# The first two down-projection tiles moved into the pools of the stage before, and four input differences moved behind the third tile's weights

## The chip, the cores and the metric

The kernel runs on one NeuronCore of a Trainium2 chip. It uses five engines that run side by side and meet only at semaphores: TensorE (PE) multiplies matrices into PSUM, ScalarE (ACT) and VectorE (DVE) work on elements, GpSimd (POOL) and SyncE (SP) here mostly issue DMAs. The metric is the device time of one execution in microseconds, the median of several runs.

## The reference

One decoder layer on 512 prompt tokens and 32 sample tokens (544 columns in all), width 1024. What matters here is its last part, the MLP with 4096 hidden units; the two mixers before it (a state-space branch and a gated recurrence) are not touched.

```python
x = x + rms_norm(merged @ w_out, norm_mix_post)
h2 = rms_norm(x, norm_mlp_pre)
m = jnp.square(jax.nn.relu(h2 @ w_up)) @ w_down
x = x + rms_norm(m, norm_mlp_post)
```

All of it is float32.

## The kernel before, in words

**A product in three passes.** Activations and weights are held transposed, 128 features per partition. Each fp32 operand is cut into a high part (ScalarE casts it to the matmul's format) and a low part (VectorE subtracts the high part from the original). A product is then high times high, high times low and low times high, added up in PSUM. So each weight tile of 128x1024 needs three steps before TensorE can use it: a DMA of 512 KB (`wt`), a cast on ScalarE (`wh`) and a subtraction on VectorE (`wl`). A full output tile has 8 operand chunks, 3 passes and 2 halves of 272 columns: 48 matmuls, in 24 pairs.

**The MLP in chunks.** The hidden units come in four chunks of 1024. The first is made in the plain way: up projections u0 to u7 of `h2x`, each followed by relu and square, cut into `a0h` and `a0l` (eight operands, 0 to 7). Then come the eight down tiles d0_0 to d0_7 of this chunk, whose results are copied from PSUM into `ov`. The chunks after it are made with a Strassen-like scheme: sums and differences of weight quarters (names A, S12, S34, B) times sums and differences of input quarters. The input's part of that are four differences of quarters of `ov`, which holds the normalized `h2` until the copies of the down tiles overwrite it. Each difference has 128x1088 elements and is cut into high and low parts: `tb[1]` (t1h, t1l), `tb[2]` (t2h, t2l), `tb[3]` (in the place of bh and bl of the second half) and `tb[4]` (t).

**Pools.** The stage up to u7 takes its weights from pool `wts` (three load buffers `wt`, two each of `wh` and `wl`) and pool `res`. When these end, pool `up` takes their memory: six load buffers, four `wh` and four `wl`. A tile of `up` that lies over a tile of an older pool waits until that one is no longer used. PSUM has two tiles for full outputs, taken in turn, so a tile's first matmul waits until the result two tiles before has been copied out.

**Order.** Up to u7 a scheduler orders each engine's work by data and priorities (`tc.high_priority`). From the differences on, the order of all five queues is that of the code (`tc.manual_schedule`). In the code before, d0_0 and d0_1 are loaded and cut from pool `up` ahead of that block (L1401 to L1406), the four differences follow, and two of them are written in place into `ov`. The splits of tb[3] and tb[4] come before d0_1's matmuls, those of tb[1] and tb[2] after.

Of the kernel before, what the change touches and what calls it, by code (L numbers as in the profile page):

```python
# [9 lines left out]
F32 = mybir.dt.float32  # L10
F32R = mybir.dt.float32r
# [34 lines left out]
def layer(ctx, tc, a, o):  # L46
# [113 lines left out]
    def views(t):  # L160
        return [(halves(hi), halves(lo)) for hi, lo in t]
# [977 lines left out]
    with tc.tile_pool(name="res", bufs=5, reuse_waits="tile") as rp:  # L1139
# [92 lines left out]
        for k in (6, 7):  # L1232
# [4 lines left out]
            with tc.high_priority(offset=EAHEAD):  # L1237
                act_full(ps, k, f"u{k}")
        nc.gpsimd.dma_start(out=x1_d, in_=x1)
    wts.close()  # L1240
    ax = views(ah_)

# [2 lines left out]


    with tc.tile_pool(name="up", bufs=1, reuse_waits="tile") as up:
        tb = {n: tuple(up.tile([P, 4, HT], F32R, tag=f"t{n}{p}", name=f"t{n}{p}") for p in "hl") for n in (1, 2)}  # L1250
        tb[3] = hb[1, 0]
        t4 = big.tile([P, 2, 4, HT], F32R, tag="yhg", name="t4")
        tb[4] = (t4[:, 0], t4[:, 1])
        flat = lambda z: z.rearrange("p a b -> p (a b)")

        def raw(src, name):
            t = up.tile([P, 1024], F32, tag="wt", name=f"wt_{name}", bufs=6)
            if src is not None:
                nc.sync.dma_start(out=t, in_=src)
            return t  # L1260

# [111 lines left out]
        def d_load(c, m):  # L1373
            src = flat(a["w_down"][c, m]) if c < 3 else a["w_down2"][0, m].rearrange("p a b c -> p (a b c)")
            D[c, m] = raw(src, f"d{c}_{m}")

        def d_cut(c, m):
            D[c, m] = cut(D[c, m], f"d{c}_{m}")
# [19 lines left out]
            else:  # L1398
                tt(mv, ps[:, :, 0:HT], mv, ADD)

        with tc.high_priority(offset=WAHEAD):  # L1401
            for m in range(2):
                d_load(0, m)
                d_cut(0, m)
                d_rest(0, m)
            d_load(0, 2)  # L1406
        with tc.manual_schedule(engines={ET.PE, ET.Activation, ET.DVE, ET.SP, ET.Pool}):

            f11, f21, f12, f22 = (ov[:, 4 * kh:4 * kh + 4, HF[hf]] for hf in range(2) for kh in range(2))
            tt_ = [up.tile([P, 4, HT], F32, tag="t", name=f"tt{i}", bufs=2) for i in range(2)]  # L1410
            tt(tt_[0], f11, f12, SUB)
            stt(tt_[1], tt_[0], -1.0, f22, MUL, SUB)
            tt(f12, f22, f12, SUB)
            stt(f21, tt_[1], -1.0, f21, MUL, SUB)
            d_part(0, 0, *range(8))
            split(*tb[3], f12)
            split(*tb[4], f21)
            d_part(0, 1, *range(8))
            d_load(0, 3)
            d_cut(0, 2)  # L1420
            d_rest(0, 2)
            split(*tb[1], tt_[0])
            d_out(0, 0)
            split(*tb[2], tt_[1])
            d_out(0, 1)
            for c in range(3):

                ms = range(2 if c == 0 else 0, 8)
                q = 4 * c + 4
                nxt = {3: [lambda: load_a(q), lambda: load_s12(q), lambda: load_s34(q), lambda: load_b(q)],  # L1430
                       5: [lambda: add_s(q), lambda: hi("A", q), lambda: lo("A", q), lambda: load_a(q + 1)],
                       6: [lambda: hi("S12", q), lambda: lo("S12", q), lambda: load_s12(q + 1)],
                       7: [lambda: hi("B", q), lambda: lo("B", q), lambda: load_s34(q + 1), lambda: load_b(q + 1)]}
                for m in ms:
                    if m + 2 < 8 and not (c == 0 and m + 2 < 4):
                        d_load(c, m + 2)
                    if m + 1 < 8:
                        if m and not (c == 0 and m + 1 < 3):
                            d_cut(c, m + 1)
                            d_rest(c, m + 1)  # L1440
                    if c == 0 or m > 1:
                        d_part(c, m, *range(8))
                    elif m == 0:
                        d_part(c, 1, *range(6))
                        d_part(c, 0, 6, 7)
                    else:
                        d_part(c, 1, 6, 7)
                    for f in nxt.get(m, ()):
                        f()
                    d_out(c, m)  # L1450

                P1(q)
                keep("c1", q)
                P2(q)
                res(q)
                hi("S34", q)
                lo("S34", q)
                hi("A", q + 1)
                c11(q)
                lo("A", q + 1)  # L1460
                P5(q)
                load_a(q + 2)
                for p in range(q, q + 4):
                    n, nn, e = p + 1 < q + 4, p + 2 < q + 4, p == q + 3
                    P6(p)
                    if p > q:
                        hi("B", p)
                        act_hi(p - 1, 0)
                        lo("S34", p)
                    keep("u2", p)  # L1470
                    if p > q:
                        lo("B", p)
                        act_lo(p - 1, 0)
                    if nn:
                        load_s12(p + 2)
                    if n:
                        P1(p + 1)
                        keep("c1", p + 1)
                        add_s(p + 1)
                    if nn:  # L1480
                        load_s34(p + 2)
                        load_b(p + 2)
                    if not n:
                        d_part(c + 1, 0, 0, 1)
                    P7(p)
                    keep("u3", p)
                    c22(p)
                    if n:
                        hi("S12", p + 1)
                        P2(p + 1)  # L1490
                        res(p + 1)
                        c11(p + 1)
                        lo("S12", p + 1)
                    else:
                        d_part(c + 1, 0, 2, 3)
                    row1_a(p)
                    if nn:
                        hi("A", p + 2)
                    if not n:
                        d_cut(c + 1, 1)  # L1500
                        d_rest(c + 1, 1)
                    P4(p)
                    row1_b(p)
                    if nn:
                        lo("A", p + 2)
                    P3(p)
                    act_hi(p, 1)
                    c12(p)
                    row0(p)
                    if p + 3 < q + 4:  # L1510
                        load_a(p + 3)
                    if n:
                        hi("S34", p + 1)
                        P5(p + 1)
                    act_lo(p, 1)
                    if p == q + 1:
                        d_load(c + 1, 0)
                    if p == q + 2:
                        d_load(c + 1, 1)
                        d_cut(c + 1, 0)  # L1520
                        d_rest(c + 1, 0)
                act_hi(q + 3, 0)
                act_lo(q + 3, 0)
                if c < 2:
                    d_part(c + 1, 0, 4, 5)

            wd = []
            xr = {}
            w47 = big.tile([P, 4, 2, 512], F32R, tag="yhg", name="wd47")
            for m in range(8):  # L1530
                t = mp.tile([P, 2, 512], F32R, tag=f"bl{m // 2}{m % 2}", name=f"wd{m}") if m < 4 else w47[:, m - 4]
                wd.append((t[:, 0], t[:, 1]))
            wt = {}
            for m in range(8):
                j = m // 2
                if m % 2 == 0:
                    if j < 2:
                        d_load(3, j + 2)
                    if 0 < j < 3:
                        d_cut(3, j + 1)  # L1540
                        d_rest(3, j + 1)
                    wt[j] = raw(a["w_down2"][1, j].rearrange("p a b c -> p (a b c)"), f"e{j}")
                if m:
                    d_part(3, m, *range(4))
                if m % 2:
                    for i in range(2):
                        split(*wd[m - 1 + i], wt[j][:, 512 * i:512 * i + 512])
                d_out(3, m)
                if m > 3:
                    hf, kh = divmod(m - 4, 2)  # L1550
                    xr[hf, kh] = mp.tile([P, 4, HT], F32, tag=f"bh{hf}{kh}", name=f"xr{hf}{kh}")
                    nc.sync.dma_start(out=xr[hf, kh], in_=x1_d[:, 4 * kh:4 * kh + 4, HF[hf]])
# [152 lines left out]
```

## Time and profile before

| | |
|---|---|
| median of three runs | 980.4 us (980.24 to 983.28) |
| profiled execution, its own time | 980.57 us |
| its span, first to last instruction | 978.5 us |
| TensorE busy | 950.3 us, 97% of the span |
| VectorE busy | 621.5 us, 64% |
| ScalarE busy | 446.1 us, 46% |
| GpSimd busy | 62.5 us, 6% |
| mean granted TensorE clock | 0.991 of full speed |
| moved by DMA | 121.26 MB, 124 GB/s on average |

Of the profiled execution's time 2.1 us lie outside the span. Busy shares are averages over the whole program; what a stage waits for is read from that stage. In timelines, a bracket at a row's end gives the idle time of the engine just before it and what ended it. Matmul ends are modelled, so the step from one pair of matmuls to the next is read from their starts.

### The profile page before, as it was taken

How to read it: one execution, taken by the hardware profiler on the slowest of the kernel's cores; microseconds unless marked ns; L12 is line 12 of the kernel's file. 1: busy time of each engine (PE TensorE's matmuls, PEld its weight loads, DVE VectorE, ACT ScalarE, POOL GpSimd, SP SyncE). 2: the span in 40 equal slices, each digit the busy share in tenths (PEclk: the TensorE clock that was granted, in tenths of full speed). 3: DMA queues.
4: the chain of work that ended last, by engine and by line, in shares of the span. 5: the costliest groups of instructions: out<-in, count | busy, mean ns of one | idle time of the engine just before them, and what ended most of it. 6: DMA issues, size and time to landing. Idle time of an engine off the chain costs nothing.

```text
span 978.5 us, 21347 instructions
## 1 busy us (share of the span) xinstructions
PE 950.3 (97%) x9120; PEld 927.0 (95%) x9120; DVE 621.5 (64%) x1158; ACT 446.1 (46%) x834; POOL 62.5 (6%) x104
## 2 busy tenths in 40 slices
PE   8999999999999999999999999889999999999995
PEld 5999999989999999999999999889999999999994
DVE  6877669496684867657458567443564476347747
ACT  6744363544536323563334566333463165216623
POOL 2100000000000000612100000000100110010000
PEclk9999999999999999999999999989999999999998
DMA  7342242141423437565422512334453454346502
GB/s 257 97 134 68 65 149 76 65 137 59 143 67 103 135 131 262 189 211 181 137 88 87 191 28 111 130 98 113 111 176 98 119 144 132 103 119 166 184 2 91
DMA packets 45406, 121.26 MB, mean 124 GB/s; under 512 B 9120, under 2 KB 12576, under 8 KB 44672
## 3 DMA queue, kind: packets, MB, share of 16 engines
q1 hardware_dynamic: 37664, 97.20, 30.4%
q0 software_dynamic: 7360, 22.15, 8.8%
q8 instruction: 71, 1.16, 0.5%
q10 hardware_dynamic: 288, 0.56, 0.2%
q14 instruction: 23, 0.19, 0.1%
HBM read 101.66 MB, written 17.06 MB: 121 GB/s over the span
## 4 chain that ended last, share of the span: by engine, by line
PE 91%; DVE 4%; ACT 2%; issue 1%; DMA 1%; SPq 0%; DVEq 0%; ACTq 0%
PE ps_in L116 27%; PE ps_d L116 17%; PE ps_u L1311 7%; PE ps_u L126 7%; PE ps_bh L116 5%; PE ps_uy L1311 4%; PE ps_o L116 2%; PE ps_e L126 2%; PE ps_o L126 2%; PE ps_bs L116 2%; PE psL L643 2%; PE ps_uz L1311 2%; PE ps_u L116 1%; PE psO L709 1%; PE psK L693 1%
## 5 line engine op out<-in xcount | busy, mean ns | idle before, releaser
L116 PE MATMUL ps_in<-hh,wh_in 128*128 128x272 f32 x736 | 159.2, 297 | 0.0
L116 PE MATMUL ps_in<-hl,wh_in 128*128 128x272 f32 x736 | 153.0, 289 | 0.0
L116 PE MATMUL ps_in<-hh,wl_in 128*128 128x272 f32 x736 | 152.3, 288 | 0.0
L116 PEld LDWEIGHTS ps_in<-hh,wh_in 128*128 128x128 f32 x736 | 115.4, 189 | 2.9 <-issue 1.6
L116 PEld LDWEIGHTS ps_in<-hl,wh_in 128*128 128x128 f32 x736 | 115.7, 189 | 0.0
L116 PEld LDWEIGHTS ps_in<-hh,wl_in 128*128 128x128 f32 x736 | 115.6, 188 | 0.0
L71 DVE TENSOR_TENSOR wl_in<-wt_in,wh_in 128x1024 fp32r<-128x1024 f32 (+1 forms) x54 | 61.6, 1143 | 60.5 <-ACT wh_in L99 58.0
L116 PE MATMUL ps_d<-a0h,wl_d 128*128 128x272 f32 x448 | 94.5, 293 | 4.8 <-DVE wl_d L71 4.8
L116 PE MATMUL ps_d<-a0h,wh_d 128*128 128x272 f32 x448 | 94.0, 291 | 3.6 <-ACT wh_d L1264 3.2
L116 PE MATMUL ps_d<-a0l,wh_d 128*128 128x272 f32 x448 | 94.5, 293 | 0.0
L99 ACT CAST wh_in<-wt_in 128x1024 fp32r<-128x1024 f32 x46 | 48.3, 1052 | 98.0 <-PE ps_in L116 93.5
L116 PEld LDWEIGHTS ps_d<-a0h,wl_d 128*128 128x128 f32 x448 | 71.3, 190 | 6.0 <-DVE wl_d L71 5.7
L116 PEld LDWEIGHTS ps_d<-a0h,wh_d 128*128 128x128 f32 x448 | 71.4, 191 | 4.0 <-ACT wh_d L1264 3.4
L116 PEld LDWEIGHTS ps_d<-a0l,wh_d 128*128 128x128 f32 x448 | 71.5, 192 | 0.0
L71 DVE TENSOR_TENSOR ov<-ps_d,ov 128x544 f32<-128x544 f32 x24 | 17.4, 724 | 61.7 <-PE ps_d L116 61.7
L71 DVE TENSOR_TENSOR wl_d<-wt_d,wh_d 128x1024 fp32r<-128x1024 f32 x28 | 34.1, 1219 | 27.0 <-ACT wh_d L1264 27.0
L1264 ACT CAST wh_d<-wt_d 128x1024 fp32r<-128x1024 f32 x28 | 29.1, 1046 | 29.6 <-PE ps_d L116 23.6
L71 DVE TENSOR_TENSOR wl_S<-wt_S,wh_S 128x1024 fp32r<-128x1024 f32 x24 | 29.3, 1219 | 11.4 <-ACT wh_S L1264 11.4
L1264 ACT CAST wh_S<-wt_S 128x1024 fp32r<-128x1024 f32 x24 | 25.2, 1050 | 10.1 <-PE ps_d L116 10.1
L676 DVE COPY_PREDICATED scT<-masks,psL 32x128 f32<-32x128 uint8 x80 | 28.3, 354 | 2.3 <-PE psS L646 0.2
L116 PE MATMUL ps_bh<-yl,wh_bh 128*128 128x272 f32 x128 | 26.8, 291 | 1.4 <-DVE yl L71 1.4
L116 PE MATMUL ps_bh<-yh,wh_bh 128*128 128x272 f32 x128 | 27.1, 293 | 0.0
(546 smaller groups left out, 2324.9 us busy)
## 6 DMA issues: line engine op xcount, KB each, us to landing
wt_in<-in_w_in SPq DMA_DIRECT2D x52, 512.0 KB, 3.6
wt_d<-in_w_down SPq DMA_DIRECT2D x28, 512.0 KB, 3.9
wt_A<-in_w_up SPq DMA_DIRECT2D x12, 512.0 KB, 4.0
wt_S<-in_w_up SPq DMA_DIRECT2D x24, 256.0 KB, 2.7
wt_S<-in_w_up POOLq DMA_DIRECT2D x24, 256.0 KB, 4.4
s<-in_hg_s SPq DMA_DIRECT2D x8, 512.0 KB, 4.3
out_hg_s<-s SPq DMA_DIRECT2D x8, 512.0 KB, 3.7
wt_bh<-in_w_br_hg SPq DMA_DIRECT2D x8, 512.0 KB, 3.5
```

Source lines behind the costliest of these rows:

```text
L71: (e or V).tensor_tensor(out=out, in0=x, in1=y, op=op)
L99: S.copy(wh, wt)
L116: mm(ps[:, i, 0:int(np.prod(x[i].shape[1:]))], lhsT=w[:, c], rhs=x[i], start=st, stop=sp)
L126: mm(ps[:, i, 0:HT], lhsT=ws[i][j][:, c], rhs=x[hf], start=st, stop=sp)
L643: mm(pq[sq * y:sq * y + m, 4 * i + w], lhsT=k[:, i, c:c + m], rhs=up(c, c + sq, i), start=True, stop=True)
L676: V.copy_predicated(blocks(sc[r], h)[:, :, y, :, 1], masks[r, L].rearrange("p x (n h) -> p x n h", h=h), pq[r].rearrange("p x (n h) -> p x ...
L693: mm(pk[:, w], lhsT=kt2[:, i, w], rhs=vt[:, i, w], start=True, stop=True)
L709: mm(po[:, w], lhsT=sc[:, i, c], rhs=vt[:, i, w], start=True, stop=(w == 0))
L1264: S.copy(h, t)
L1311: mm(ps, lhsT=w[:, c], rhs=x_[:, k], start=(first and k == 0 and j == 0), stop=(k == 3 and j == 2), skip_group_check=True)
```

## The change

The first two down tiles, d0_0 and d0_1, are loaded, cut and multiplied in the stage of the older pools, with the helper `weights` that serves u6 and u7, right behind u7. Their matmuls keep their place. In the manual block their PSUM tiles are only taken over; the third tile's cut is written first, then the four differences. None of these is written in place any more: the first two keep their buffers (tag `t`), the third and fourth take two of the six load buffers of `up`, which grow from 1024 to 1088 columns. The copy of d0_0 comes before the split of tb[3], that of d0_1 before the split of tb[4], and the splits of tb[1] and tb[2] come in the rounds of the third and fourth tile.

```diff
+        ax = views(ah_)
+        first_d = []
+        for m in range(2):
+            wh, wl = weights(a["w_down"][0, m], f"d0_{m}")
+            first_d.append(dense_tile(f"ps_d0_{m}"))
+            dense(first_d[m], wh, wl, ax)
     wts.close()
-    ax = views(ah_)
...
         def raw(src, name):
-            t = up.tile([P, 1024], F32, tag="wt", name=f"wt_{name}", bufs=6)
-            if src is not None:
+            t = up.tile([P, 1088], F32, tag="wt", name=f"wt_{name}", bufs=6)
+            if src is not False:
+                t = t[:, 0:1024]
+            if src is not None and src is not False:
...
-        with tc.high_priority(offset=WAHEAD):
+        tb = {3: hb[1, 0]}
+        with tc.manual_schedule(engines={ET.PE, ET.Activation, ET.DVE, ET.SP, ET.Pool}):
             for m in range(2):
-                d_load(0, m)
-                d_cut(0, m)
-                d_rest(0, m)
-            d_load(0, 2)
-        with tc.manual_schedule(engines={ET.PE, ET.Activation, ET.DVE, ET.SP, ET.Pool}):
-
-            f11, f21, f12, f22 = (ov[:, 4 * kh:4 * kh + 4, HF[hf]] for hf in range(2) for kh in range(2))
-            tt_ = [up.tile([P, 4, HT], F32, tag="t", name=f"tt{i}", bufs=2) for i in range(2)]
-            tt(tt_[0], f11, f12, SUB)
-            stt(tt_[1], tt_[0], -1.0, f22, MUL, SUB)
-            tt(f12, f22, f12, SUB)
-            stt(f21, tt_[1], -1.0, f21, MUL, SUB)
-            d_part(0, 0, *range(8))
-            split(*tb[3], f12)
-            split(*tb[4], f21)
-            d_part(0, 1, *range(8))
-            d_load(0, 3)
+                PD[0, m] = first_d[m]
+                d_load(0, m + 2)
             d_cut(0, 2)
             d_rest(0, 2)
-            split(*tb[1], tt_[0])
+
+            f11, f21, f12, f22 = (ov[:, 4 * kh:4 * kh + 4, HF[hf]] for hf in range(2) for kh in range(2))
+            tf = {n: up.tile([P, 4, HT], F32, tag="t", name=f"tf{n}", bufs=2) for n in (1, 2)}
+            for n in (3, 4):
+                tf[n] = raw(False, f"tf{n}").rearrange("p (a b) -> p a b", a=4)
+            tt(tf[1], f11, f12, SUB)
+            stt(tf[2], tf[1], -1.0, f22, MUL, SUB)
+            tt(tf[3], f22, f12, SUB)
+            stt(tf[4], tf[2], -1.0, f21, MUL, SUB)
             d_out(0, 0)
-            split(*tb[2], tt_[1])
+            split(*tb[3], tf[3])
...
             d_out(0, 1)
+            split(*tb[4], tf[4])
...
+                    if c == 0 and m < 4:
+                        split(*tb[m - 1], tf[m - 1])
                     d_out(c, m)
```

How this moves the instructions is seen on three queues. ScalarE first, from the end of u6 on, before the change: `t_u` is the relu of an up tile (first u6's, then u7's), `a0h` its cast, `wh_d` the casts of the down tiles' weights, `bh`, `t` and `t1h` the high parts of the differences.

```order
L1205 ACTIVATE t_u_7975<-ps_u_7926 128x544
L1219 ACTIVATE e_7250<-psv_7992,eps_v 128x272
L132 CAST a0h_7263<-t_u_7975 128x544
L1205 ACTIVATE t_u_8050<-ps_u_8001 128x544
L132 CAST a0h_7265<-t_u_8050 128x544
L1264 CAST wh_d_0_8068<-wt_d_0_8066 128x1024
L132 CAST bh_6965<-ov 128x1088
L1264 CAST wh_d_1_8074<-wt_d_1_8072 128x1024
L132 CAST t_8065<-ov 128x1088
L1264 CAST wh_d_2_8192<-wt_d_2_8078 128x1024
L132 CAST t1h<-tt_8082 128x1088
L1397 COPY ov<-ps_d_0_8088 128x544
```

And ScalarE from the same place after the change:

```order
L99 CAST wh_d_0_8058<-wt_d_0_8056 128x1024
L1205 ACTIVATE t_u_7975<-ps_u_7926 128x544
L1219 ACTIVATE e_7250<-psv_7992,eps_v 128x272
L132 CAST a0h_7263<-t_u_7975 128x544
L99 CAST wh_d_1_8113<-wt_d_1_8111 128x1024
L1205 ACTIVATE t_u_8050<-ps_u_8001 128x544
L132 CAST a0h_7265<-t_u_8050 128x544
L1267 CAST wh_d_2_8177<-wt_d_2_8173 128x1024
L1400 COPY ov<-ps_d_0_8062 128x544
L132 CAST bh_6965<-wt_tf_8183 128x1088
L1400 COPY ov<-ps_d_1_8117 128x544
L132 CAST t_8192<-wt_tf_8184 128x1088
```

The casts of d0_0 and d0_1 moved ahead of the relus of u6 and u7, the third tile's cast follows a0h of u7 directly, and the two copies out of PSUM now stand ahead of the splits of the third and fourth difference.

VectorE from the last square of the up stage on, before the change: `t_u` is the square of u7, `a0l` its low part, `tt` and `ov` the four differences, `wl_d` the low parts of the down tiles' weights.

```order
L71 TENSOR_TENSOR t_u_8050<-t_u_8050 128x544
L71 TENSOR_TENSOR a0l_7266<-t_u_8050,a0h_7265 128x544
L71 TENSOR_TENSOR tt_8082<-ov 128x1088
L74 SCALAR_TENSOR_TENSOR tt_8083<-tt_8082,ov 128x1088
L71 TENSOR_TENSOR ov<-ov 128x4x272
L74 SCALAR_TENSOR_TENSOR ov<-tt_8083,ov 128x4x272
L71 TENSOR_TENSOR wl_d_0_8070<-wt_d_0_8066,wh_d_0_8068 128x1024
L71 TENSOR_TENSOR bl_6966<-ov,bh_6965 128x1088
L71 TENSOR_TENSOR wl_d_1_8076<-wt_d_1_8072,wh_d_1_8074 128x1024
```

VectorE after the change, with two more rows at the start that were not between the squares before:

```order
L71 TENSOR_TENSOR wl_d_0_8059<-wt_d_0_8056,wh_d_0_8058 128x1024
L71 TENSOR_TENSOR t_u_7975<-t_u_7975 128x544
L71 TENSOR_TENSOR a0l_7264<-t_u_7975,a0h_7263 128x544
L71 TENSOR_TENSOR wl_d_1_8114<-wt_d_1_8111,wh_d_1_8113 128x1024
L71 TENSOR_TENSOR t_u_8050<-t_u_8050 128x544
L71 TENSOR_TENSOR a0l_7266<-t_u_8050,a0h_7265 128x544
L71 TENSOR_TENSOR wl_d_2_8179<-wt_d_2_8173,wh_d_2_8177 128x1024
L71 TENSOR_TENSOR tf_8181<-ov 128x1088
L74 SCALAR_TENSOR_TENSOR tf_8182<-tf_8181,ov 128x1088
L71 TENSOR_TENSOR wt_tf_8183<-ov 128x1088
L74 SCALAR_TENSOR_TENSOR wt_tf_8184<-tf_8182,ov 128x1088
L71 TENSOR_TENSOR bl_6966<-wt_tf_8183,bh_6965 128x1088
```

The low parts of the first two tiles moved ahead of the squares of u6 and u7, and that of the third tile stands between a0l of u7 and the four differences.

SyncE's queue of loads after the change, from the load of u7's weights on, with what each load waits for (DMAHW and DMASW are counts of hardware and software DMA queues, PE, DVE and Pool counts of engines). Before, the loads of d0_0 to d0_5 stood in the same order, all six in pool `up`.

```order
L96 DMA wt_u_7995<-in_w_up 128x1024 [waits DMAHW4_49,DVE_49]
L96 DMA wt_d_0_8056<-in_w_down 128x1024 [waits DMAHW5_49,DVE_49]
L96 DMA wt_d_1_8111<-in_w_down 128x1024 [waits DMAHW6_49,DVE_49]
L1262 DMA wt_d_2_8173<-in_w_down 128x1024 [waits PE_49]
L1262 DMA wt_d_3_8175<-in_w_down 128x1024 [waits DMASW1_49,DMASW5_49,DMASW0_49,PE_49]
L1262 DMA wt_d_4_8200<-in_w_down 128x1024 [waits DMASW5_49,DMASW6_49,DMASW3_49,DMASW7_49,DMASW0_49,Pool_49]
L1262 DMA wt_d_5_8258<-in_w_down 128x1024 [waits DMASW4_49]
```

The first two loads are now of line 96, the older pool's; the order of the queue is the same.

## Rows read from the trace of the kernel before

**Rows 1.** The page: busy us, share of the span and instructions of TensorE.

```profile
PE 950.3 (97%) x9120; PEld 927.0 (95%) x9120; DVE 621.5 (64%) x1158; ACT 446.1 (46%) x834; POOL 62.5 (6%) x104
```

**Rows 2.** TensorE's waits, whole run: who waited for whom: us, times, longest.

```profile
PE ps_bh L116 <- DVE yl L71: 1.4, 1, 1.4
...
PE ps_d L116 <- DVE ov L71: 0.4, 1, 0.4
```

**Rows 3.** The chain that ended last: start us, us, what.

```profile
639.83 50.43 PE ps_d L116 x380
```

**Rows 4.** TensorE's timeline, 630 to 645: start us, us, line, operation, tiles.

```profile
630.38 0.41 PE L116 MATMUL ps_u<-bh,wl_u 128*128 128x272 f32 x2
633.95 0.62 PE L116 MATMUL ps_d<-a0h,wh_d 128*128 128x272 f32 x2 [3.15 <-ACT wh_d L1264]
634.37 0.66 PE L116 MATMUL ps_d<-a0l,wh_d 128*128 128x272 f32 x2
639.83 0.82 PE L116 MATMUL ps_d<-a0h,wl_d 128*128 128x272 f32 x2 [4.80 <-DVE wl_d L71]
...
644.08 0.59 PE L116 MATMUL ps_d<-a0h,wl_d 128*128 128x272 f32 x2
644.50 0.41 PE L116 MATMUL ps_d<-a0h,wh_d 128*128 128x272 f32 x2
```

**Rows 5.** Stretches: PE, PEld, DVE, ACT, POOL busy; granted clock, DMA share, GB/s.

```profile
430.00:440.00 10.00, 8.61 (x112) 8.12 (x110) 8.21 (x13) 9.73 (x17) 0.54 (x1) 1.00 0.92 342
...
636.00:640.00 4.00, 0.17 (x1) 0.17 (x2) 4.00 (x5) 2.53 (x3) 0.00 (x0) 0.50 0.00 0
640.00:644.50 4.50, 4.50 (x20) 4.50 (x21) 4.50 (x5) 2.47 (x3) 0.00 (x0) 0.51 0.55 176
644.50:650.00 5.50, 5.50 (x46) 5.50 (x45) 1.70 (x2) 1.61 (x2) 1.74 (x2) 1.00 0.70 164
```

**Rows 6.** ScalarE's timeline, 630 to 654.

```profile
630.89 0.62 ACT L1205 ACTIVATE t_u<-ps_u 128x544 f32<-128x544 f32 x1 [4.39 <-PE ps_u L116]
632.31 0.65 ACT L132 CAST a0h<-t_u 128x544 fp32r<-128x544 f32 x1 [0.79 <-DVE t_u L71]
632.86 1.04 ACT L1264 CAST wh_d<-wt_d 128x1024 fp32r<-128x1024 f32 x1
...
647.74 0.61 ACT L1397 COPY ov<-ps_d 128x544 f32<-128x544 f32 x1 [5.26 <-PE ps_d L116]
...
653.82 0.61 ACT L1397 COPY ov<-ps_d 128x544 f32<-128x544 f32 x1 [4.47 <-PE ps_d L116]
```

**Rows 7.** VectorE's timeline, 606 to 675.

```profile
606.60 1.23 DVE L71 TENSOR_TENSOR wl_u<-wt_u,wh_u 128x1024 fp32r<-128x1024 f32 x1 [3.40 <-ACT wh_u L99]
...
631.55 0.73 DVE L71 TENSOR_TENSOR t_u<-t_u 128x544 f32<-128x544 f32 x1 [4.29 <-ACT t_u L1205]
632.99 0.73 DVE L71 TENSOR_TENSOR a0l<-t_u,a0h 128x544 fp32r<-128x544 f32 x1 [0.71 <-ACT a0h L132]
633.63 1.28 DVE L71 TENSOR_TENSOR tt<-ov 128x1088 f32<-128x1088 f32 x1
634.95 1.29 DVE L74 SCALAR_TENSOR_TENSOR tt<-tt,ov 128x1088 f32<-128x1088 f32 x1
...
638.56 1.22 DVE L71 TENSOR_TENSOR wl_d<-wt_d,wh_d 128x1024 fp32r<-128x1024 f32 x1
...
674.79 1.41 DVE L71 TENSOR_TENSOR wt_S<-wt_S,wt_A 128x512 f32<-128x512 f32 x2
```

**Rows 8.** SyncE's timeline (six loads of wt_d).

```profile
617.68 2.81 SPq L1259 DMA_DIRECT2D wt_d<-in_w_down  x6
```

**Rows 9.** Landing of the up weights (tile wt_u).

```profile
DMA to landing us min/median/max: 3.4/4.3/4.5
```

**Rows 10.** Landing of the down weights, 600 to 660 (tile wt_d).

```profile
DMA to landing us min/median/max: 3.5/5.7/8.1
```

**Rows 11.** The page's DMA issues: operation, count, KB, median us to landing.

```profile
wt_S<-in_w_up POOLq DMA_DIRECT2D x24, 256.0 KB, 4.4
```

More of the change, by code (lines that the diff above doesn't have):

```diff
@@ L1239, in layer @@
         nc.gpsimd.dma_start(out=x1_d, in_=x1)
+        ax = views(ah_)
[4 more added lines that the diff above has]
+            dense(first_d[m], wh, wl, ax)
     wts.close()
-    ax = views(ah_)
     with tc.tile_pool(name="up", bufs=1, reuse_waits="tile") as up:
[L1250 to L1253, printed above, removed]
         flat = lambda z: z.rearrange("p a b -> p (a b)")
         def raw(src, name):
-            t = up.tile([P, 1024], F32, tag="wt", name=f"wt_{name}", bufs=6)
-            if src is not None:
+            t = up.tile([P, 1088], F32, tag="wt", name=f"wt_{name}", bufs=6)
+            if src is not False:
+                t = t[:, 0:1024]
+            if src is not None and src is not False:
                 nc.sync.dma_start(out=t, in_=src)
@@ L1399, in d_out @@
                 tt(mv, ps[:, :, 0:HT], mv, ADD)
-        with tc.high_priority(offset=WAHEAD):
+        tb = {3: hb[1, 0]}
+        with tc.manual_schedule(engines={ET.PE, ET.Activation, ET.DVE, ET.SP, ET.Pool}):
             for m in range(2):
-                d_load(0, m)
-                d_cut(0, m)
-                d_rest(0, m)
-            d_load(0, 2)
-        with tc.manual_schedule(engines={ET.PE, ET.Activation, ET.DVE, ET.SP, ET.Pool}):
-            f11, f21, f12, f22 = (ov[:, 4 * kh:4 * kh + 4, HF[hf]] for hf in range(2) for kh in range(2))
-            tt_ = [up.tile([P, 4, HT], F32, tag="t", name=f"tt{i}", bufs=2) for i in range(2)]
-            tt(tt_[0], f11, f12, SUB)
-            stt(tt_[1], tt_[0], -1.0, f22, MUL, SUB)
-            tt(f12, f22, f12, SUB)
-            stt(f21, tt_[1], -1.0, f21, MUL, SUB)
-            d_part(0, 0, *range(8))
-            split(*tb[3], f12)
-            split(*tb[4], f21)
-            d_part(0, 1, *range(8))
-            d_load(0, 3)
+                PD[0, m] = first_d[m]
+                d_load(0, m + 2)
             d_cut(0, 2)
             d_rest(0, 2)
-            split(*tb[1], tt_[0])
+            f11, f21, f12, f22 = (ov[:, 4 * kh:4 * kh + 4, HF[hf]] for hf in range(2) for kh in range(2))
[6 more added lines that the diff above has]
+            stt(tf[4], tf[2], -1.0, f21, MUL, SUB)
             d_out(0, 0)
-            split(*tb[2], tt_[1])
+            split(*tb[3], tf[3])
+            t4 = big.tile([P, 2, 4, HT], F32R, tag="yhg", name="t4")
+            tb[4] = (t4[:, 0], t4[:, 1])
             d_out(0, 1)
+            split(*tb[4], tf[4])
+            for n in (1, 2):
+                tb[n] = tuple(up.tile([P, 4, HT], F32R, tag=f"t{n}{p}", name=f"t{n}{p}") for p in "hl")
             for c in range(3):
```

## The prediction

> **What bounds the kernel now.** I read the busy shares first. TensorE is busy for 950.3 of 978.5 us [rows 1], so the question is where it is not. Next came its waits over the whole run: besides the two below, the ones that matter here are small, 1.4 us in an earlier stage and 0.4 us near the end [rows 2]. The chain of waits then shows TensorE alone for long stretches, and one of these begins at 639.83 with the down projection [rows 3]. TensorE's own timeline around that point gives the two large waits: 3.15 us before the first pair of down matmuls, put down to ScalarE's cast wh_d, and 4.80 us before the third pair, put down to VectorE's wl_d [rows 4]. The stretches tell what else happened there: the granted clock is 0.50 and 0.51 from 636 to 644.5 us, which is the 1.2 GHz level, and 1.00 again after it, 2.4 GHz [rows 5]. So this one seam, from the last up projection (u7) to the first down tile (d0_0), costs two waits and a slow stretch.
>
> Why it waits is read from the other two engines. ScalarE does relu and cast of u7 first, with VectorE's square between them, and casts d0_0's weights only at 632.86, for 1.04 us [rows 6]. The cast is done at 633.90, but VectorE begins the low part wl_d at 638.56: the four differences of the input, 633.63 to 638.56, stand ahead of it in its queue [rows 7]. The weights themselves had been requested at 617.68 and landed at most 8.1 us later [rows 8, 10]; memory is not what is late.
>
> **The change, part by part.** *The time that can go.* The last pair of u7 matmuls starts at 630.38, pairs follow each other by 0.253 us (two copies of finished tiles stand 653.82 - 647.74 = 6.08 us apart, 24 pairs a tile [rows 6]), so TensorE could go on at 630.63. It is back at full pace at 644.50. In between it did 12 pairs: two from 633.95 and ten from 639.83 to 644.08 [rows 4], worth 12 x 0.253 = 3.04 us at full pace. Lost: 644.50 - 630.63 - 3.04 = 10.83 us. Of that 3.15 + 4.80 = 7.95 are waits, and the remaining 2.88 is work at half clock and the restart.
>
> The half-clock part can also be weighed by a rule. Ten pairs take 644.50 - 639.83 = 4.67 us there, and the clock had fallen while TensorE waited [rows 4, 5]. The Trainium skill (TensorE: Matmul & The Clock Gate, Part 1) says that the throttled clock is the default state which activity releases, and prices a throttled stretch at its length times one minus the clock ratio. By that the term is an estimated 2.3 us and the sum 10.3; the trace has 2.88, because the two pairs at 633.95 and the restarts are in it as well, and I keep the trace's.
>
> *Can the two tiles start at once?* The first two tiles' weights now use the older pool's three load buffers. d0_0's load waits for wl_u5, d0_1's for wl_u6, which starts at 606.60 and lasts 1.23 us [rows 7]; a load of this size in that pool landed in 4.5 us at most [rows 9], so both are there by 613, 17 us early. Their split needs the buffers of u6 and u7. For d0_0 that is the end of u6, 6 us before use, and nothing else wants the engines. For d0_1 the cast waits for the last use of u7's weights, and it now stands on ScalarE ahead of u7's relu, and its low part on VectorE ahead of u7's square. That is the one place where the change puts work into a chain which TensorE will wait for: a0h7 and a0l7, the eighth operand of d0_0. In whole durations, from 630.89 where the relu stood: cast 1.04, relu 0.62 (632.55); VectorE's low part 1.22 ends at 633.2, then the square 0.73 (633.9), cast 0.65 (634.6), low part 0.73: 635.4 with the hops [rows 6, 7]. TensorE asks for a0h7 after 21 pairs, 630.63 + 5.32 = 635.95, and for a0l7 a pair later, 636.2. Margin 0.8 us; cost nothing.
>
> *The third tile.* ScalarE casts d0_2 after a0h7, to 635.65, VectorE makes its low part to 636.9, and only then the four differences. The four took 638.56 - 633.63 = 4.93 us before [rows 7]; the third ends after three quarters of that and its own drain, 3.8 us: 640.7. The copy that empties d0_0's PSUM writes where those differences read, so it waits for the third: 640.7 + 0.61 = 641.3 [rows 6]. TensorE wants that PSUM for d0_2 after 48 pairs, at 630.63 + 12.16 = 642.79. Margin 1.4 us. Queued behind the waiting copy on ScalarE are the cast of the third difference and the next copy, which needs d0_1's end anyway. After that copy (about 643.5) come the cast of the fourth difference, 1.11 by its columns from the 1.04 above, and d0_3's cast, 1.04, then its low part, 1.22: 647.2 against 630.63 + 72 x 0.253 = 648.9 when TensorE gets there. Margin 1.7 us. With this hidden, the differences cost TensorE nothing; with the cover gone they cost what stands over the margin.
>
> *Loads behind.* The third tile's load is the first in the new pool. In the built program its wait is for a TensorE count that the second normalization's sum reaches, long before; it is issued right behind d0_1's, near 608. The fourth's waits for the last use of u5's weights, which is the event that freed all six loads at 617.68 before [rows 8]. Two load buffers now hold the third and fourth differences, so the first strip of the next stage (S12, S34) waits for the splits of those, near 643 and 646. Its landing through two queues, 4.4 us for the second leg [rows 11] and about as much for the first, puts it at some 655. VectorE first adds there at 674.79 before [rows 7], which becomes 664. Covered by 9 us.
>
> *The sum.* 980.57 (profiled execution: span 978.5 and 2.1 around it) - 10.83 = 969.74. The median of the runs shown, 980.4, lies 0.17 lower: 969.6 us. Behind 644.50 TensorE is the chain, so what is won at this seam stays won. Uncertainty of the term: its pieces are read to a few hundredths; clock and restart could leave up to half a microsecond more in place, or a like amount less by run spread: 968.9 to 970.4.
>
> **The rivals.** *A, a smaller wait stays.* One of the three margins, 0.8, 1.4 or 1.7 us, does not hold, because an instruction behind a waiting one cannot overtake. For it: exactly this is seen in the trace, wl_d held for 4.7 us behind the differences although its cast was done [rows 7]. Against: full durations were used and instructions overlap a little at their ends. Price: 1 us if just missed; at most a 3 us wait with the 2.88 of half clock on top. The wait of 1.4 us at 435 left the clock at 1.00 [rows 2, 5], so a short one costs itself alone. Time 970.6 to 975.5, most likely 971.5. The Trainium skill (PSUM — Partial Sum Buffer, Engine vs sequencer instructions) states such queues for ScalarE and VectorE as strictly first in, first out, which speaks against putting a cast with an open wait ahead of the relu; the wl_d row agrees with it.
>
> *B, slower.* The third tile's load cannot land while the first two tiles' weights are in use, because the new pool lies over the old one. Then it is issued at d0_1's end, 642.8, and everything that now stands behind it in order is late with it: landing 3.5 to 8.1 us [rows 10], cast 1.04, low part 1.22, three differences 3.8, copy 0.61, together 10.2 to 14.8 us of wait, and 2.88 of half clock. Net of 10.83 that is 2.2 to 6.8 slower, 982.6 to 987.2, at the middle 985. It decides from a landing after about 644 us. For it: the waits before were of just this sort, loads freed all together at 617.68. Against: the count that the load waits for, as told above.
>
> *C, given back later.* The strips of the next stage are late, or a transfer already hidden turns out to set a later wait, so that 2 to 10 of the 10.83 us come back: 972 to 980.4. For it: the two buffers lent to the differences. Against: 9 us of cover, and no TensorE wait but 0.4 us in the 280 us up to the last projection.
>
> **How the numbers follow.** My forecast gets 0.80, A 0.10, B 0.04, C 0.06, of which 0.04 ends within no change. About 0.3% (3 us) is what a measurement of this kernel can tell from no change. Faster: 0.80 + 0.10 + 0.02 = 0.92; same 0.04; slower 0.04. The range takes the forecast and most of A: 968.9 to 973.0.
>
> **What would show it.** In the changed profile TensorE's waits should no longer hold wh_d or wl_d at this seam; the granted clock should be 1.00 from 625 on and its mean above 0.991; the copies of the first three tiles should stand at about 641, 643 and 649, the last two some 6 us apart; the span should be near 967.7. A wait on a0h or a0l near 636 or on the copy near 643 would be A; a third load issued after 640 would be B; a new wait in the next stage C. A time above 973 makes the prediction wrong.

## The result and the profile after

The changed kernel takes 971.26 us (median of 4 runs, 969.6 to 971.94), the kernel before 981.84 us beside it (4 runs, 980.24 to 984.63). The ratio is 0.9887, 95% interval 0.9857 to 0.9917: 1.1% faster. The profiled execution took 971.8 us, its span is 969.7 us.

The busy shares, as in [rows 1]. TensorE does the same work, in a span that is 8.8 us shorter.

```profile
PE 949.5 (98%) x9120; PEld 926.4 (96%) x9120; DVE 621.7 (64%) x1158; ACT 445.6 (46%) x834; POOL 62.5 (6%) x104
```

TensorE's waits over the whole run (us, times, longest), which answer to [rows 2]:

```profile
PE psL L643 <- issue: 1.9, 1, 1.9
...
PE ps_bh L116 <- DVE yl L71: 1.4, 1, 1.4
...
PE ps_d L116 <- DVE ov L71: 0.4, 1, 0.4
```

The two of 1.4 and 0.4 us are there as before; none holds wh_d or wl_d. The first, 1.9 us, stands elsewhere in the kernel and is looked at under the last two experiments.

TensorE's timeline at the seam, which answers to [rows 4]: the last pair of u7, the first of d0_0, the first pair with a0l7, and the first pair of the third tile.

```profile
632.41 0.42 PE L116 MATMUL ps_u<-bh,wl_u 128*128 128x272 f32 x2
632.67 0.41 PE L116 MATMUL ps_d<-a0h,wh_d 128*128 128x272 f32 x2
...
638.23 0.42 PE L116 MATMUL ps_d<-a0l,wh_d 128*128 128x272 f32 x2
...
644.81 0.42 PE L116 MATMUL ps_d<-a0h,wh_d 128*128 128x272 f32 x2
```

The first down pair follows the last up pair by 0.26 us, where 3.57 us lay between them before, and none of the four rows carries a wait in brackets. From 632.67 to 644.81 it is 12.14 us for 48 pairs, 0.253 each. The stretches, which answer to [rows 5] (busy us of PE, PEld, DVE, ACT, POOL, then the granted clock, DMA share and GB/s):

```profile
630.00:636.00 6.00, 6.00 (x50) 6.00 (x49) 2.39 (x3) 1.98 (x3) 0.00 (x0) 1.00 0.01 3
636.00:640.00 4.00, 4.00 (x33) 4.00 (x33) 3.47 (x4) 1.19 (x2) 0.00 (x0) 1.00 0.17 25
640.00:644.50 4.50, 4.50 (x38) 4.50 (x37) 3.96 (x4) 1.62 (x2) 0.00 (x0) 1.00 0.24 95
```

TensorE is busy throughout and the clock is 1.00, the 2.4 GHz level, where it was 0.50 and 0.51. The chain has the whole down projection in one piece again, but from 632.83 instead of 639.83 [rows 3]:

```profile
632.83 48.63 PE ps_d L116 x384
```

ScalarE's timeline, which answers to [rows 6]. The first tile's cast (626.15) now stands ahead of u6's relu, the second tile's (632.61) ahead of u7's relu, the third tile's behind u7's cast; the copy of the first tile waited until VectorE's third difference (tile wt_tf) was written.

```profile
626.15 1.05 ACT L99 CAST wh_d<-wt_d 128x1024 fp32r<-128x1024 f32 x1 [3.15 <-PE ps_u L116]
...
632.61 1.05 ACT L99 CAST wh_d<-wt_d 128x1024 fp32r<-128x1024 f32 x1 [2.84 <-PE ps_u L116]
633.57 0.62 ACT L1205 ACTIVATE t_u<-ps_u 128x544 f32<-128x544 f32 x1
635.59 0.65 ACT L132 CAST a0h<-t_u 128x544 fp32r<-128x544 f32 x1 [1.41 <-DVE t_u L71]
636.15 1.04 ACT L1267 CAST wh_d<-wt_d 128x1024 fp32r<-128x1024 f32 x1
642.27 0.61 ACT L1400 COPY ov<-ps_d 128x544 f32<-128x544 f32 x1 [5.08 <-DVE wt_tf L71]
...
645.01 0.61 ACT L1400 COPY ov<-ps_d 128x544 f32<-128x544 f32 x1 [1.13 <-PE ps_d L116]
...
651.09 0.61 ACT L1400 COPY ov<-ps_d 128x544 f32<-128x544 f32 x1 [2.52 <-PE ps_d L116]
...
657.17 0.61 ACT L1400 COPY ov<-ps_d 128x544 f32<-128x544 f32 x1 [3.52 <-PE ps_d L116]
```

VectorE's timeline, which answers to [rows 7]: the second tile's low part, u7's last low part, the third tile's low part, the last of the four differences, the fourth tile's low part, and the first addition of the next stage.

```profile
633.70 1.23 DVE L71 TENSOR_TENSOR wl_d<-wt_d,wh_d 128x1024 fp32r<-128x1024 f32 x1 [3.17 <-ACT wh_d L99]
...
636.27 0.72 DVE L71 TENSOR_TENSOR a0l<-t_u,a0h 128x544 fp32r<-128x544 f32 x1 [0.71 <-ACT a0h L132]
637.22 1.23 DVE L71 TENSOR_TENSOR wl_d<-wt_d,wh_d 128x1024 fp32r<-128x1024 f32 x1 [0.22 <-ACT wh_d L1267]
...
642.10 1.28 DVE L74 SCALAR_TENSOR_TENSOR wt_tf<-tf,ov 128x1088 f32<-128x1088 f32 x1
...
647.87 1.22 DVE L71 TENSOR_TENSOR wl_d<-wt_d,wh_d 128x1024 fp32r<-128x1024 f32 x1
...
665.99 1.41 DVE L71 TENSOR_TENSOR wt_S<-wt_S,wt_A 128x512 f32<-128x512 f32 x2
```

SyncE's loads, which answer to [rows 8]: the first two tiles in the older pool, four in the new one, and then the two strips of the next stage.

```profile
589.48 20.74 SPq L96 DMA_DIRECT2D wt_d<-in_w_down  x2
610.26 10.77 SPq L1262 DMA_DIRECT2D wt_d<-in_w_down  x4
...
645.23 0.33 SPq L1283 DMA_DIRECT2D wt_S<-in_w_up  x1
647.98 0.33 SPq L1288 DMA_DIRECT2D wt_S<-in_w_up  x1
```

How long these six loads of wt_d took to land, which answers to [rows 10]:

```profile
DMA to landing us min/median/max: 3.4/4.1/5.5
```

**Where the time came from.** The stretch from the last pair of u7 to the copy of the third down tile holds the whole seam and is free of what came before it. Before, it ends with this row of ScalarE's timeline:

```profile
659.90 0.61 ACT L1397 COPY ov<-ps_d 128x544 f32<-128x544 f32 x1 [4.52 <-PE ps_d L116]
```

That is 659.90 - 630.38 = 29.52 us before and 651.09 - 632.41 = 18.68 us after, 10.84 us less. The two profiled executions differ by only 980.57 - 971.8 = 8.8 us, since that of the changed kernel reached the seam 632.41 - 630.38 = 2.03 us later. After the third copy the two run alike: copies 6.08 us apart in both, the next stage's first addition 8.8 us earlier (665.99 against 674.79).

### The profile page after: what moved, and what is told of

The parts are those of the page before. It is cut to its first block, busy times and chain, and to the rows that moved or that the text cites. A ratio compares the mean times of both kernels' runs of the same rounds, so it can differ in the third digit from the quotient of the medians.

```text
span 969.7 us, 21346 instructions
## 1 busy us (share of the span) xinstructions
PE 949.5 (98%) x9120; PEld 926.4 (96%) x9120; DVE 621.7 (64%) x1158; ACT 445.6 (46%) x834; POOL 62.5 (6%) x104
## 4 chain that ended last, share of the span: by engine, by line
PE 92%; DVE 4%; ACT 2%; issue 1%; DMA 1%; SPq 0%; DVEq 0%; ACTq 0%
PE ps_in L116 27%; PE ps_d L116 17%; PE ps_u L1314 7%; PE ps_u L126 7%; PE ps_bh L116 5%; PE ps_uy L1314 4%; PE ps_o L116 3%; PE ps_e L126 2%; PE ps_o L126 2%; PE ps_bs L116 2%; PE psL L643 2%; PE ps_uz L1314 2%; PE ps_u L116 1%; PE psO L709 1%; PE psK L693 1%
## 5 line engine op out<-in xcount | busy, mean ns | idle before, releaser
L1267 ACT CAST wh_d<-wt_d 128x1024 fp32r<-128x1024 f32 x26 | 27.0, 1047 | 29.6 <-PE ps_d L116 18.1
```

What stands on the lines that cost most here:

```text
L1267: S.copy(h, t)
```

## The experiments

All figures of the seam are of this stretch, in the profiled execution of each kernel:

```
kernel            last pair of u7   third copy   stretch   against before
before                  630.38        659.90      29.52
changed                 632.41        651.09      18.68       -10.84
differences first       631.64        650.32      18.68       -10.84
order alone             630.77        654.61      23.84        -5.68
clock kept              632.42        659.90      27.48        -2.04
one tile                632.74        651.42      18.68       -10.84
short wait              631.80        650.89      19.09       -10.43
long wait               632.71        654.24      21.53        -7.99
changed, again          632.73        651.41      18.68       -10.84
before, again           632.22        661.29      29.07        -0.45
```

**Differences first.** The changed kernel with the third tile's cut behind the four differences.

```diff
-            d_cut(0, 2)
-            d_rest(0, 2)
...
             stt(tf[4], tf[2], -1.0, f21, MUL, SUB)
+            d_cut(0, 2)
+            d_rest(0, 2)
             d_out(0, 0)
```

> The changed kernel with the four differences back ahead of the third tile's low part on VectorE; the first two tiles stay in the older pools. Theory (the gain is the first two tiles' weights being ready at the end of u7, and the place of the differences matters only while they stand ahead of a low part that TensorE is waiting for): the four differences end some 5 us after a0l of u7, at about 642 in the changed kernel's trace, the third tile's low part at 643.1, and TensorE wants it at 645.3, so no wait and a ratio to before of 0.989, as the changed kernel. Rival (the place behind the third tile's weights carries part of the gain): TensorE waits for wl_d of d0_2 by 1 us or more, ratio 0.990 to 0.995.

Measured: 970.73 us (5 runs), ratio 0.9888 (0.9871 to 0.9905). The copy of the first tile comes earlier against the last pair of u7, at 8.40 us (640.04 - 631.64) instead of 9.86, by ScalarE's timeline:

```profile
640.04 0.61 ACT L1400 COPY ov<-ps_d 128x544 f32<-128x544 f32 x1 [3.63 <-DVE wt_tf L71]
```

There is no wait, and the stretch is the same. The order of the differences and the third tile moves slack between two waits that are both covered; it carries nothing of the gain.

**Order alone.** The kernel before, in its own pools, with the first two tiles' loads and cuts put into the block of fixed order, ahead of the differences.

```diff
-        with tc.high_priority(offset=WAHEAD):
+        with tc.manual_schedule(engines={ET.PE, ET.Activation, ET.DVE, ET.SP, ET.Pool}):
             for m in range(2):
...
             d_load(0, 2)
-        with tc.manual_schedule(engines={ET.PE, ET.Activation, ET.DVE, ET.SP, ET.Pool}):
```

> The kernel before with the order alone changed: the cuts of d0_0 and d0_1 come ahead of the four differences, everything still in the new pool, where the casts cannot be placed ahead of u7's relu. Theory: the wait for wh_d of 3.15 us stays, the one for wl_d shrinks from 4.80 to about 0.5 us, and the clock still falls in the first wait, costing some 1.7 us: about 5.4 of the 10.8 us come back, 975 us at a before of 980.4, ratio 0.9945. Rival (the order of VectorE's queue is the whole of it): 970, ratio 0.989. Second rival (the older pools are the whole of it): no change, 1.000.

Measured: 976.28 us (6 runs), ratio 0.9943 (0.9928 to 0.9957). The wait for wl_d is gone, that for wh_d stays at the very length of [rows 4], as TensorE's timeline shows:

```profile
634.33 0.76 PE L116 MATMUL ps_d<-a0h,wh_d 128*128 128x272 f32 x2 [3.15 <-ACT wh_d L1264]
```

The stretches of this kernel (columns as above):

```profile
631.00:636.00 5.00, 1.79 (x8) 1.30 (x7) 3.14 (x4) 3.17 (x4) 0.00 (x0) 0.84 0.00 0
636.00:640.00 4.00, 4.00 (x27) 4.00 (x27) 3.96 (x4) 0.00 (x0) 0.00 (x0) 0.77 0.59 198
640.00:644.50 4.50, 4.50 (x38) 4.50 (x37) 4.50 (x5) 3.97 (x4) 0.89 (x1) 1.00 0.33 54
```

The clock is lower until 640 only. The stretch is 5.68 us shorter than before and 5.16 us longer than in the changed kernel; of these 3.15 are the wait and 2.01 the rest, the slow stretch above all. So the gain has two parts that come from two places: the differences' place in VectorE's queue, some 5.7 us, and, as what is left, the older pools, which put the cast of the first tile ahead of u6's relu, some 5.2 us. This run also shows that one wait of 3.15 us, without the second, is followed by the lower clock.

**Clock kept.** The kernel before, with matmuls whose result nobody reads filling most of both waits (20 ahead of the first down pair, 32 ahead of the third).

```diff
-            d_part(0, 0, *range(8))
+            fill(20)
...
+            fill(32)
...
+            d_part(0, 0, *range(1, 8))
```

> The kernel before with idle TensorE time filled: 20 matmuls of 128x272 into an unused PSUM tile ahead of the first down matmul, 32 more ahead of the third pair; they use operands that are there and their result is not read. Both fills are shorter than the waits (2.5 of 3.15 us, 4.05 of 4.80 us). Theory (of the 10.83 us, 2.88 are half clock and restart): the granted clock stays at 1.00 through 636 to 644.5, the waits stay, the real work is done in 3.04 instead of 5.9 us, 2.5 to 2.9 us come back: 977.7 at a before of 980.4, ratio 0.997. Rival (the slow stretch is no cost of its own, the end is set by VectorE's and ScalarE's work there): no change, 1.000.

Measured: 979.72 us (12 runs), ratio 0.9981 (0.9967 to 0.9995). TensorE's timeline with the fill:

```profile
632.42 0.41 PE L116 MATMUL ps_u<-bh,wl_u 128*128 128x272 f32 x2
632.67 2.68 PE L1419 MATMUL ps_fill<-a0h 128*128 128x272 f32 x20
635.99 0.52 PE L1426 MATMUL ps_d<-a0h,wh_d 128*128 128x272 f32 x2 [0.65 <-ACT wh_d L1264]
...
641.87 0.52 PE L1429 MATMUL ps_d<-a0h,wl_d 128*128 128x272 f32 x2 [1.09 <-DVE wl_d L71]
```

The two stretches in which the clock had been 0.50 and 0.51:

```profile
636.00:640.00 4.00, 4.00 (x32) 4.00 (x32) 3.96 (x4) 0.48 (x1) 0.00 (x0) 1.00 0.00 0
640.00:644.50 4.50, 3.41 (x28) 3.19 (x27) 4.50 (x5) 4.50 (x5) 0.00 (x0) 1.00 0.33 105
```

The down pairs start as late as before (635.99 - 632.42 = 3.57 us after the last up pair, third pair 5.88 us after the first, both as in [rows 4]), but the clock is 1.00 and the third copy follows the third pair after 659.90 - 641.87 = 18.03 us instead of 659.90 - 639.83 = 20.07. So the clock alone is 2.04 us. The rest of the 2.88 is read off starts. The bracket of a wait begins at the modelled end of the pair ahead of it, and in [rows 4] these pairs end 0.41 and 0.66 us after their start (the second at the lower clock), where the next could have started after 0.253: 0.16 and 0.41 us, together 0.57, are lost to the waits too, though no bracket counts them. The other 0.27 or so is the slower start of the pairs behind the two waits. The time is 2.0 us below the kernel before; the expectation had 2.5 to 2.9, since it put all of the 2.88 on the clock.

**One tile.** The changed kernel with only the first tile in the older pools; the second is loaded in the new pool and cut ahead of the differences, the third behind the split of tb[3].

```diff
-        for m in range(2):
+        for m in range(1):
             wh, wl = weights(a["w_down"][0, m], f"d0_{m}")
...
+            for m in range(1, 4):
+                d_load(0, m)
+            d_cut(0, 1)
+            d_rest(0, 1)
+            d_part(0, 1, *range(8))
...
             split(*tb[3], tf[3])
+            d_cut(0, 2)
+            d_rest(0, 2)
```

> Only d0_0 in the older pools; d0_1 is loaded and cut in the new pool, its low part ahead of the differences, the third tile's cut behind them. Theory (what counts is that each tile's weights are ready when TensorE comes to it, and one tile of cover, 6.1 us, is enough for the next): d0_1's cast at about 635.6, low part done near 637, wanted at 638.6; the third tile's low part done near 644.7, wanted at 645.3: ratio 0.989 as the changed kernel, with 0.5 us of margin; at worst a wait under 1 us, 0.990. Rival (both tiles are needed in the older pools): a wait of 2 us or more at d0_1 or d0_2, ratio 0.992 or more.

Measured: 972.19 us (6 runs), ratio 0.9897 (0.9878 to 0.9915), stretch 18.68 us, no wait at the seam. One tile in the older pools is enough; the second one's place there is worth nothing that can be measured.

**Short wait and long wait.** The changed kernel, with u7's relu written four or eight times more (the diff is that of the first; the second has 8 for 4). Its values stay; what stands behind it on ScalarE and VectorE comes later.

```diff
-            S.activation(t, ps[:, :, 0:HT], AF.Relu)
+            for _ in range(1 + 4 * (k - 6)):
+                S.activation(t, ps[:, :, 0:HT], AF.Relu)
```

> The changed kernel with the relu of the last tile of hidden parts written four times more to the same tile (the values are the same), some 0.52 us each by the row of that relu: the last tile's two parts come about 2.1 us later. In the changed kernel the first down pair asks for the low part with 1.2 us to spare (asked 238.2 after 600, ready 237.0), so TensorE should now stand for about 0.9 us at the last group of the first down tile. Theory (a short wait costs only itself, as rival A of the prediction priced it below 1.4 us): the granted clock stays 1.00 behind the wait, and from the last pair of the up projection to the copy of the third down tile it is 18.68 + 0.9 = 19.6 us; the kernel is about 1 us slower than the changed one, 0.990 of the kernel before. Rival (every wait in this chain costs the clock too): the granted clock falls to about 0.5 for some microseconds and the stretch takes 21 to 22 us, 0.992.

(The two times that this expectation names, 238.2 and 237.0, are 638.23 and 636.99 in the changed kernel's profile.)

Measured: 971.13 us (4 runs), ratio 0.9888 (0.9871 to 0.9904). The wait is smaller than expected, because the program's scheduler set two pairs of the second tile between those with a0h7 and a0l7, which TensorE's timeline shows as x4:

```profile
637.68 0.77 PE L116 MATMUL ps_d<-a0h,wh_d 128*128 128x272 f32 x4 [0.17 <-ACT a0h L132]
638.29 0.67 PE L116 MATMUL ps_d<-a0l,wh_d 128*128 128x272 f32 x4
```

u7's low part starts 637.66 - 631.80 = 5.86 us after the last up pair instead of 636.27 - 632.41 = 3.86, so 2.0 us later; the stretch grows by 0.41 us. Most of the 2.0 went into the margin of 1.24 us, the rest into those two pairs and a wait. The granted clock stayed at 1.00 (636 to 650 us). The five relus took 3.24 us, so a repeat was some 0.65 us and not 0.52; part of that is not seen in u7's low part, since the square had stood behind the second tile's low part on VectorE.

> The same with eight relus more, some 4.1 us: TensorE should stand for about 2.9 us at the last group of the first down tile. Theory (a wait as long as the one of 3.15 us before the change costs itself and a stretch at the lower clock, 2.88 us for the two of 3.15 and 4.80 together, 2.0 of it given back when the clock was kept up by fill): the granted clock falls behind the wait, and the stretch from the last pair of the up projection to the third copy is 18.68 + 2.9 + 1 to 2 = 22.6 to 23.6 us; about 4 to 5 us slower than the changed kernel, 0.993 to 0.994 of the kernel before. Rival (the wait costs only itself): 21.6 us, granted clock 1.00, 0.9915.

Measured: 973.78 us (4 runs), ratio 0.9917 (0.9902 to 0.9932). The stretch, 21.53 us, and the ratio are what the rival had (21.6 and 0.9915), but not in its way: there is no single wait of 2.9 us. TensorE's timeline has two shorter ones:

```profile
638.02 0.41 PE L116 MATMUL ps_d<-a0h,wl_d 128*128 128x272 f32 x2
639.79 0.52 PE L116 MATMUL ps_d<-a0h,wh_d 128*128 128x272 f32 x2 [1.36 <-ACT t_u L1206]
640.14 0.41 PE L116 MATMUL ps_d<-a0l,wh_d 128*128 128x272 f32 x2
...
647.87 0.52 PE L116 MATMUL ps_d<-a0h,wh_d 128*128 128x272 f32 x2 [0.96 <-ACT ov L1401]
```

The stretches that begin behind the first wait and hold the second:

```profile
640.00:644.50 4.50, 4.50 (x37) 4.49 (x37) 3.56 (x4) 1.60 (x2) 0.00 (x0) 1.00 0.02 7
644.50:650.00 5.50, 4.54 (x37) 4.32 (x36) 4.93 (x5) 2.80 (x4) 0.00 (x0) 1.00 0.28 89
```

The scheduler put the second tile's first groups ahead of the late a0h7. Those write the PSUM tile that u7 had used (the pool has two), and wait for the last relu to empty it, 1.36 us. The second wait, 0.96 us, is for the copy of the first tile: the differences are late too, so the third difference holds it. The second is one that the prediction had named under rival A, the copy; the first, on PSUM, it had not named. The clock stays 1.00 behind each. Together they cost 21.53 - 18.68 = 2.85 us, 0.26 each over the 2.32 in their rows. Of that, 0.16 is the wait's too, left out by the bracket (the pair at 638.02 lasts 0.41 to its modelled end, where the next could have started after 0.253), and 0.10 the slower pair behind the wait (640.14 - 639.79 = 0.35 instead of 0.253). The theory's fall of the clock was not put to the test at its length, and the rival, a wait that costs no clock, holds for these two.

**Both kernels again.** No edit; one profile each.

> The changed kernel once more, unchanged, for one profile. In its first profile TensorE stood 1.91 us for 'issue' at 207 us and ran at half clock behind it, and was 2.03 us later than the kernel before when it reached the last pair of the up projection (632.41 against 630.38). Theory (this is spread from run to run, not a part of the change): the wait is of another length here, and the last pair of the up projection moves with it, anywhere from 630.3 to 632.8; from there to the third copy it is 18.68 us again. Rival (it belongs to this build, as its instructions lie differently): 1.9 us again, half clock behind it, 632.4.

> The kernel before once more, unchanged, for one profile. In its first profile the wait for 'issue' at 207 us was 1.23 us and the granted clock stayed 1.00. Theory (spread from run to run): another length, and the last pair of the up projection anywhere from 630.3 to 632.8; from there to the third copy 29.52 us again. Rival (it belongs to the build): 1.23 us again, 630.4.

Measured: 972.06 and 981.74 us, one run each; another run of the kernel before beside them took 985.18. The wait in question, from TensorE's timeline of four profiles. First the changed kernel:

```profile
207.44 0.21 PE L643 MATMUL psL<-qp,k 128*32 128x16 f32 x3 [1.91 <-issue]
```

The changed kernel again:

```profile
207.72 0.21 PE L643 MATMUL psL<-qp,k 128*32 128x16 f32 x3 [2.20 <-issue]
```

The kernel before:

```profile
206.89 0.21 PE L643 MATMUL psL<-qp,k 128*32 128x16 f32 x3 [1.23 <-issue]
```

The kernel before again:

```profile
207.24 0.21 PE L643 MATMUL psL<-qp,k 128*32 128x16 f32 x3 [1.91 <-issue]
```

The kernel before, which had 1.23 us and an undisturbed clock, now has 1.91 us, and behind it this stretch, at a granted clock of 0.50:

```profile
209.00:211.00 2.00, 2.00 (x10) 2.00 (x10) 1.96 (x5) 0.41 (x1) 0.00 (x0) 0.50 0.97 391
```

Its last pair of u7 comes at 632.22, 1.84 us later than in its first profile. So nearly all of the 2.03 us by which the changed kernel reached the seam later can come without the change, in a kernel that had not had it in another run. The changed kernel itself was seen with the long wait only, twice; differences first, which is nearly the same kernel, had 1.23 us. The changed kernel's stretch is 18.68 again; that of the kernel before is 29.07, 0.45 less than expected. Its down pairs start at the same distances (first at 635.78, 3.56 us after the last up pair, third 5.88 us later), and the third copy follows the third pair after 19.63 us instead of 20.07, so what differs is the slow stretch. The term of the change is therefore known to about half a microsecond, 10.4 to 10.8.

## Why the prediction was right

**The sum.** The term of 10.83 us came out as 10.84 in the stretch. That it did so to the hundredth is luck: with the second profile of the kernel before it is 29.07 - 18.68 = 10.39. The 2.88 us beside the two waits were put down to half clock and restart together, and that reading is not quite right: the fill shows 2.04 of clock, 0.57 belongs to the waits and stands outside their brackets, and some 0.27 is the slower start behind them. The sum does not change by it. The Trainium skill (TensorE: Matmul & The Clock Gate, Part 1) gave an estimated 2.3 for the throttled stretch alone; the fill's 2.04 is nearer to that than the whole 2.88 is. The prediction's sum was safe because it took the total from the timeline and not from a rule for a part of it.

**The time.** 969.6 us was forecast and 971.26 measured. The ratio that was implied, 969.6 / 980.4 = 0.989, is the measured one. The step that was a little off is the starting point: the three runs shown had a median of 980.4, the runs beside the changed kernel 981.84, and 17 of the kernel before in the first four experiments 981.75. The first profile of the kernel before had the short wait at 207 us.

**The margins.** All three held, and were somewhat wider than worked out from whole durations. a0l7 was written at 636.27 + 0.72 = 636.99 and asked for at 638.23: 1.24 us against 0.8. The first tile's copy ended at 642.88, and the third tile began at 644.81: 1.93 against 1.4. The fourth tile's low part ended at 649.09, and the 72 pairs end at 632.67 + 72 x 0.253 = 650.9: 1.8 against 1.7. The repeats of the relu show the first two to be real: used up, they turned into a wait of 0.17 us for a0h7 (short wait) and one of 0.96 us for the copy (long wait). The third was not tried.

**The copies.** Forecast at about 641, 643 and 649; with the 2.03 us taken off they stand at 640.2, 643.0 and 649.1.

**Rival A** did not come about in the changed kernel. The long wait shows its mechanism (what stands behind a waiting instruction waits too: the copy, held by the late third difference) and its price for a short wait, nearly: waits of 1.36 and 0.96 us left the clock at 1.00, but cost 0.26 us each over their rows. **Rival B** fell: the four loads in the new pool went out between 610.26 and 621.03, over 11 us before the end of u7, and all landed within 5.5 us. **Rival C** fell: the two strips were issued at 645.23 and 647.98, where 643 and 646 plus the shift were forecast, and the first addition came 8.82 us after the fourth tile's copy (665.99 - 657.17), as it did before, so TensorE's chain and not the loads sets it. No new wait of TensorE follows. (Its range, 972 to 980.4, belongs to some 2.4 to 10.8 us given back; the 2 to 10 that it names would be 971.6 to 979.6.)

**What the prediction did not separate** is which part of the change matters. The order on VectorE alone gives half of it, the older pools for one tile the other half, and the order of third tile and differences nothing. That the differences are no longer written in place, and the earlier copies, were not tried apart. No version tried is clearly faster than the changed kernel: the three nearest have ratios of 0.9888, 0.9888 and 0.9897 with intervals that overlap its own.

## What to carry to other kernels

Where an engine waits, sum the whole stretch from its last useful instruction to its return to full pace, and take off the work in it at full pace; waits, clock and restart are then all in, while the brackets and the clock alone would have come to 7.95 + 2.04 = 9.99 us of the 10.83. Look for whose queue the needed small instruction stands in, since here both waits were instructions of 1.0 to 1.2 us behind other work, with their data in place. Compare two profiles from a mark just ahead of the change, not by their spans: here the spans differ by 8.8 us and the seam by 10.84.

## What was not expected of the hardware

TensorE's wait for "issue" near 205 us, which no semaphore in the trace explains, was 1.23 to 2.20 us long in ten profiles of eight kernels, none of which has other code there. In the four where it was 1.23, 1.23, 1.49 and 1.55 us (before, differences first, order alone, clock kept) the granted clock stayed at 1.00 behind it; in the six where it was 1.90 to 2.20 us the clock fell to about 0.5, the 1.2 GHz level, for some microseconds. In the changed kernel seven pairs then took 3.17 us, from 209.34 to 212.51 on its timeline, instead of 7 x 0.253 = 1.77:

```profile
209.34 0.65 PE L116 MATMUL ps_in<-hh,wh_in 128*128 128x272 f32 x2
...
212.51 0.41 PE L116 MATMUL ps_in<-hl,wh_in 128*128 128x272 f32 x2
```

That is 1.4 us, and the row behind the wait stands 0.55 us later than in the first profile of before (207.44 against 206.89): 1.95 of the 2.03 us. What makes the wait longer or shorter stays open.

Nor is this wait all that differs from run to run. Differences first and clock kept came to the first matmul of this group 1.23 us later than the kernel before (206.14 against 204.91). They had lost it by 17 us. In the kernel before the granted clock was 1.00 from 6 to 15 us; in clock kept it was 0.82 from 6 to 10 and 0.81 behind that (columns as above):

```profile
10.00:15.00 5.00, 5.00 (x14) 2.47 (x12) 3.65 (x10) 3.40 (x6) 0.00 (x0) 0.81 1.05 389
```

So clock kept reached the seam as late as the changed kernel, at 632.42, although the clock stayed at 1.00 behind its wait of 1.55 us.
